# HGRN scores: levels 32 and 64 as separate products on three column groups, copied into A

## The chip, the cores and the metric

The kernel runs on one core of one Trainium2 chip. The metric is the device time of one execution in microseconds. A core has a tensor engine (PE, whose weight loads are listed apart as PEld), a vector engine (DVE), a scalar engine (ACT), GpSimd (POOL) and a sync engine (SP) that here issues the weight transfers. Each engine takes its own instructions in a fixed order, and semaphores tie the engines together.

## The reference, cut to what matters

The reference is a two-layer decoder for one sequence of 256 tokens of width 1024. Layer 0 mixes tokens with a gated linear recurrence (HGRN2), layer 1 with a three-branch sparse attention; each is followed by a SwiGLU feed-forward, and conditioning vectors made from `c` scale, shift and gate every sub-layer. The change touches the recurrence alone:

```python
def step(state, inp):
    G = jnp.cumsum(g_, axis=2)
    o_inter = einsum(q_ * exp(G), state)
    decay = where(causal, exp(G[t] - G[s]), 0)        # per key feature
    attn = einsum('bhtk,bhsk,bhtsk->bhts', q_, k_, decay)
    o_intra = einsum(attn, v_)
    new_state = exp(G_last) * state + einsum(k_ * exp(G_last - G), v_)
```

For each of 8 heads the result is one causal 256 by 256 score matrix times the values. A score of query t and key s is the sum over 128 features of q, k and the product of all decays between s and t.

## The kernel before, in words

The kernel does not run the recurrence chunk by chunk. It splits the causal triangle by levels 1, 2, 4, ..., 128. At level b the tokens are cut into blocks of 2b; queries in the second half of a block meet keys in its first half, and the decay between them is a product of one factor per key and one per query, both measured from the middle of the block. So at each level the scores are plain matrix products of a scaled key tile with a scaled query tile. `hgrn_decays` makes those tiles `X[0]` to `X[7]` (and `X[8]` for the diagonal) with exponentials on ACT (line 786, recorded under `act` at line 429) and running sums on DVE (lines 790 to 792). `hgrn_scores` (line 793) takes a group of two heads and makes the products; `hgrn_values` (line 841) multiplies by the values.

The four groups are called S0 to S3 in the written order of the stage, with D0 and D1 the decays of two groups each, `i` value products, `g` gate products, V0 and V1 the products with the values: `D0 i0 g0 S1 i1 S0 V0 D1 g1 S2 S3 i2 i3 V1`.

Inside one group there are four tiles of 128 by 128 scores on the diagonal (two heads times two halves of the tokens, index `ht`) and two tiles below it (level 128, tile `psx`, line 825). For a diagonal tile the scores inside blocks of 32 are made with 32-column products on four column groups of PE (lines 807 and 813, tile `psl`), masked and merged by DVE into `ab` (lines 827 and 834), and spread by a DVE product with a block mask into the block diagonal of `A` (line 838). Levels 64 and 32 go to a second accumulator tile, `psu`: a product of a cleared bf16 tile with itself opens the accumulation over all 128 by 128 places (line 817), then the level-64 product (line 818), two level-32 products (line 821), then a second product with the cleared tile, two columns wide, that closes the accumulation (line 824). DVE adds the whole of `psu` to `A` (line 839). ACT copies `psx` into `A[:, 4:6]` (line 840). An fp32 product shows as two weight loads and two matmuls in the trace.

Accumulators for all these (`psl`, `psu`, `psx`, `hgpv`, `hgt`, `adat`) come from one ring of four banks (`m_tile`, line 491). The order of instructions on each engine is made by a planner from the program's order, its own cost estimates and the priorities in `PRI`; the program text fixes dependencies, not the final order. Around the scores PE also runs value products (`hg_i`, lines 748 to 750), gate products (`hg_g`, lines 484 to 486) and conditioning vectors (`adapsg`, `adapsss`, line 385). Weights are streamed by SP in chunks of 1 MB, four ahead, and split into two parts by ACT (line 307, `wh`) and DVE (line 308, `wl`).

Of the kernel before, what the change touches and what calls it, by code (L numbers as in the profile page):

```python
# [21 lines left out]
S = 256  # L22
D = 1024
# [4 lines left out]
RAW = 4  # chunks loaded ahead  # L28
DEFER = 3  # chunks of a feed-forward's first product taken before rstd is there
XBUFS = 14  # L30
XMOD, XOFF = 5, 9  # every how many halves of a chunk go to the second ring, and until which chunk
PTS = 3  # pairs of heads with probabilities at a time
QACT, KACT = 0x0F, 0xF0  # chunks of the queries' and values' input made on ACT
CSTK = 7  # chunk after which the rest of the constants is loaded
# how far ahead of the program (behind it, if negative) some of the work is issued
# [7 lines left out]


# conditioning vectors (s shift and scale, g gate) on the tensor engine; the others are row sums on DVE
# [11 lines left out]
# The order of the work. hgrn: D decays, S scores, i/g products, V values. nsa: q queries, G gates, c compression,  # L57
# n norms, w values, x compressed softmax, s scores, v outputs, a conditioning chunk.
# hada, f0, f1: after how many chunks of products each conditioning chunk comes.
# [115 lines left out]
def row_constants():  # L175
    """Row 32 m + h of column block m: ones on the partitions of half h."""
    r = np.zeros((P, 4, P), np.float32)
    for m in range(4):
        for h in range(2):
            r[32 * m + h, m, 64 * h:64 * h + 64] = 1.0  # L180
    return r.reshape(P, 4 * P)


def first(name):
    """What the method issues is moved by PRI in the order of the program."""
    def wrap(f):
        def g(self, *a, **k):
            n = PRI.get(name, 0)
            if not n:
                return f(self, *a, **k)  # L190
            with self.tc.high_priority(offset=n):
                return f(self, *a, **k)
        return g
    return wrap


class K:
# [154 lines left out]
    def ada(self, kind, l, i, t):  # L352
        """Two columns of 128 conditioning values: rows of the chunk against c."""
        nc = self.nc
        m, A, bias = self.ada_tiles(l)
        c0, c1 = (i, 8 + i) if kind == "ada_ss" else (16 + 2 * i, 17 + 2 * i)
        for h, c in enumerate((c0, c1)):
            junk = self.tp.tile([P, D], F32, tag="junk", bufs=1, name="junk")
            nc.vector.tensor_tensor_reduce(out=junk, in0=t[:, h * D:(h + 1) * D], in1=self.crep, scale=1.0,  # L359
                                           scalar=0.0, op0=ALU.mult, op1=ALU.add, accum_out=m[:, c:c + 1])  # L360
        if kind == "ada_ss":
            gain = self.col(self.gain(l))
            nc.vector.scalar_tensor_tensor(A[:, i:i + 1], m[:, c1:c1 + 1], self.bias1(l)[:, c1:c1 + 1],
                                           gain[:, i:i + 1], op0=ALU.add, op1=ALU.mult)
            nc.vector.tensor_tensor(m[:, i:i + 1], m[:, i:i + 1], bias[:, i:i + 1], op=ALU.add)
            if i == 7:
                self.mods[("A", l)] = A
                self.mods[("shift", l)] = m[:, 0:8]
        else:
            nc.vector.tensor_tensor(m[:, c0:c1 + 1], m[:, c0:c1 + 1], bias[:, c0:c1 + 1], op=ALU.add)  # L370
            if i == 3:
                self.mods[("gate", l)] = m[:, 16:24]

    def ada_pe(self, kind, l, i, t):
        """c against the chunk's rows, summed over the chunks; at the last one the columns."""
# [43 lines left out]
    def act(self, out, in_, func, **kw):  # L419
        """An activation whose function lies in a table set; sets change only between phases."""  # L420
        nc = self.nc
        want = 18 if func == AF.Silu else 6
        if want != self.aset:
            load = nc.scalar.add_instruction(mybir.InstLoadActFuncSet(
                act_func_set_id=want, name=nc.get_next_instruction_name(), engine=nc.scalar.engine, ins=[], outs=[]))
            for i in self.aphase:
                self.after(load, i)
            self.aset, self.aload, self.aphase = want, load, []
        r = nc.scalar.activation(out, in_, func, **kw)  # L429
        self.after(r, self.aload)  # L430
        self.aphase.append(r)
# [6 lines left out]
    def rsqrt_cols(self, v, n, tag):  # L438
        """v ** -0.5 for a few columns, by Newton's method from the exponent."""
# [11 lines left out]
    def rsqrt(self, v, shape, tag):  # L451
        """(v + EPS) ** -0.5, one Newton step after the tables."""
# [13 lines left out]
    def sigmoid(self, out, v, shape):  # L466
        """exp(min(v, 0)) / (1 + exp(-|v|))"""
# [26 lines left out]
    def gemm(self, ps, w, hh, hl, n=256):  # L494
        """ps = sum over k of w[k] (128 x 128) against h[:, k, :n]."""
# [3 lines left out]
    def tiles(self, w):  # L499
        """The 128 x 128 tiles of half a chunk: high and low parts."""  # L500
        return [(w[0][:, e * P:(e + 1) * P], w[1][:, e * P:(e + 1) * P]) for e in range(8)]
# [6 lines left out]
    def set_shift(self, hh, hl, l):  # L508
        """Columns 256 and 257 of the moving operand: the shift vector and zeros."""
# [14 lines left out]
    def stat(self, x, m):  # L524
        """Adds the squares of chunk m to the sum over chunks."""
# [10 lines left out]
    def first_stat(self):  # L536
        """rstd of the input."""
# [25 lines left out]
    def stat_end(self, ps=None):  # L563
        """self.rstd = (mean of squares + EPS) ** -0.5 of every token, on all partitions."""
# [17 lines left out]
    def full_chunk(self, hh, hl, m, A, sh, pool):  # L582
        """Chunk m of x * rstd * A + shift, in two parts."""
# [7 lines left out]
    def full_pair(self, which, l, xr, pool, on_act):  # L591
        """The same from x * rstd."""
# [22 lines left out]
    def gemm_deferred(self, ws, h, pool, name, ub=2):  # L615
        """Products with h as it is before rstd: their values times rstd, and the shift's column."""
# [17 lines left out]
    def residual(self, ps, m, gate, nxt):  # L634
        """x_new chunk m = x + gate * y, with what the next products need of it."""
# [20 lines left out]
    def hgrn(self):  # L656
# [3 lines left out]
        with self.tc.tile_pool(name="hg", bufs=1) as gp, self.tc.tile_pool(name="hg2", bufs=2) as g2:  # L660
# [17 lines left out]
            # room of the next operands until their first parts are there  # L678
# [62 lines left out]
    def gemm_tok(self, ps, h, ws):  # L741
        """Tokens on the partitions: h (stationary) against the weights."""
# [9 lines left out]
    def hgrn_decays(self, fs, qs, g2):  # L752
        """X[l]: exp of the log decay from each block's middle; left keys, right queries. X[8]: keys."""
# [41 lines left out]
    def hgrn_scores(self, X, q, g2, i):  # L795
        nc = self.nc
        # scores inside blocks of 32, all levels side by side
# [3 lines left out]
        for h in range(2):  # L801
            for tt in range(2):
# [6 lines left out]
                for l, b in enumerate(LOW):  # L809
                    for j in range(4):  # L810
# [4 lines left out]
                                         tile_position=(0, 32 * j))  # L815
                u = psu[:, ht]
                nc.tensor.matmul(u, lhsT=self.zero, rhs=self.zero, start=True, stop=False)
                nc.tensor.matmul(u[0:64, 64:128], lhsT=X[6][:, h, base:base + 64],
                                 rhs=X[6][:, h, base + 64:base + 128], start=False, stop=False)
                for j in (0, 64):  # L820
                    nc.tensor.matmul(u[j:j + 32, j + 32:j + 64], lhsT=X[5][:, h, base + j:base + j + 32],
                                     rhs=X[5][:, h, base + j + 32:base + j + 64], start=False, stop=False,
                                     tile_position=(0, j))
                nc.tensor.matmul(u[:, 0:2], lhsT=self.zero, rhs=self.zero[:, 0:2], start=False, stop=True)
# [14 lines left out]
        nc.vector.tensor_tensor(A[:, 0:4], A[:, 0:4], psu, op=ALU.add)  # L839
# [3 lines left out]
    def hgrn_values(self, ns, As, v, g2, q):  # L843
        """Into q: rms-normalised rows of A^T v times the gain, features on the partitions."""
# [75 lines left out]
    def raw_heads(self, ps, name):  # L920
        """Products of two column tiles off the accumulator, and their squares."""
# [7 lines left out]
    def rotate(self, u, gain, swap, kr, name):  # L929
        """kr = the rotation of u times the gain: halves of a head change places."""  # L930
# [11 lines left out]
    def head_norm(self, pairs, kr, gain=None, kn=None):  # L942
        """Four column tiles: kr times the heads' rstd, kn = u times that and the gain."""
        nc = self.nc
        ps = self.m_tile([P, S], "hs")
        # rows 32 e and 32 e + 1: the two heads of column tile e
# [124 lines left out]
    def cmp_blocks(self, sw, u, kind, Dt, pool):  # L1071
        """Dt[(parity, d), i, (head, block)]: token 16 block + 2 i + parity of a head, plus its position."""
# [160 lines left out]
    def attend_values(self, j):  # L1233
# [4 lines left out]
        for half in range(2):  # L1238
            for br in range(2):
                PT[half, br] = self.pt_tile(f"PT{j}_{half}{br}")  # L1240
                pt = self.pp.tile([P, 3, P], F32, tag="acc", bufs=3, name="ptt")
                # columns: keys 0 with tokens 0, keys 0 with tokens 1, keys 1 with tokens 1
# [27 lines left out]
def _kt(w):  # L1270
    """[K, M] -> [128, K / 128, M]"""
# [3 lines left out]
def head_order():  # L1275
    """Query heads by (column tile, half): halves of a tile use key heads 2 g and 2 g + 1."""
# [107 lines left out]
```

## Time and profile before

| what | value |
|---|---|
| median of 3 runs | 765.33 us (764.39 to 766.17) |
| span of the profiled execution | 764.0 us |
| PE busy | 736.8 us, 96% of the span, 6580 products |
| DVE busy | 573.1 us, 75% |
| ACT busy | 395.2 us, 52% |
| share of the critical chain on PE | 88% |
| mean granted TensorE clock | 0.988 |

The page gives no other time for the profiled execution than its span, from the first to the last instruction. A row of the timeline gives start, duration, engine, line, operation, output and inputs, shape, count, and in brackets the idle time before it. A matmul's duration runs from its start to a modelled end, so starts that follow one another closely tell the rate, not the durations. "Issue" in the chain is time in which the engine waited for nothing that the profile shows. [...]

### The profile page before, as it was taken

What the parts mean: (1) busy time and instruction counts of PE and PEld (TensorE: products, weight loads), DVE (VectorE), ACT (ScalarE), POOL (GpSimd) and SP (SyncE); (2) the same over time, 40 slices, a digit from 0 to 9 for tenths busy, and PEclk for the clock granted to TensorE, in tenths of its full rate; (3) what the DMA queues carried; (4) which work ended last, traced back from release to release, by engine and by line L of the source; (5) the groups of instructions that cost most, each with busy time, mean ns of one, the idle gap of its engine ahead of it and who ended that gap; (6) DMA issues with size and microseconds to landing.
All of it is one profiled execution on the core that took longest, in us unless ns stands there. A gap on an engine that the chain in (4) does not pass through costs nothing.

```text
span 764.0 us, 15991 instructions
## 1 busy us (share of the span) xinstructions
PE 736.8 (96%) x6580; PEld 671.6 (88%) x6580; DVE 573.1 (75%) x1231; ACT 395.2 (52%) x746; POOL 0.6 (0%) x7
## 2 busy tenths in 40 slices
PE   3999999899999999999999899999999999999997
PEld 1999986689999999999996787555799999999997
DVE  5996988469898988987598869668489757565631
ACT  4339856357644544544474644558466444444330
POOL 0000000000000000000000000000000000000000
PEclk9999999799999999999999999999999999999999
DMA  8999745475489796887733942552755555755710
GB/s 330 335 341 355 274 133 210 139 284 203 143 320 377 275 366 266 333 333 285 274 112 97 359 134 74 173 215 109 275 204 182 208 179 206 275 203 205 266 39 21
DMA packets 26571, 174.13 MB, mean 228 GB/s; under 512 B 3201, under 2 KB 4609, under 8 KB 6018
## 3 DMA queue, kind: packets, MB, share of 16 engines
q1 hardware_dynamic: 24912, 170.80, 60.7%
q10 hardware_dynamic: 1586, 2.32, 1.1%
q8 instruction: 51, 0.84, 0.4%
q14 instruction: 22, 0.18, 0.1%
HBM read 170.48 MB, written 1.05 MB: 225 GB/s over the span
## 4 chain that ended last, share of the span: by engine, by line
PE 88%; DVE 5%; ACT 3%; DMA 2%; issue 1%; ACTq 0%; DVEq 0%
PE ff L486 11%; PE ff L485 11%; PE ff L484 11%; PE ffo L484 6%; PE ffo L485 5%; PE ffo L486 5%; PE adapsss L385 2%; PE po L1260 2%; PE ptt L1244 2%; PE s L1207 2%; DVE wl L308 1%; PE q L485 1%; PE nso L484 1%; PE hg_i L748 1%; PE hgo L484 1%; PE q L486 1%
## 5 line engine op out<-in xcount | busy, mean ns | idle before, releaser
L308 DVE TENSOR_TENSOR wl<-raw,wh 128x1024 fp32r<-128x1024 f32 x201 | 244.0, 1222 | 72.7 <-ACT wh L307 72.2
L307 ACT CAST wh<-raw 128x1024 fp32r<-128x1024 f32 x201 | 208.7, 1048 | 152.8 <-PE ff L485 53.0
L486 PE MATMUL ff<-hh,wl 128*128 128x256 f32 (+1 forms) x704 | 198.3, 282 | 0.0
L484 PE MATMUL ff<-hh,wh 128*128 128x256 f32 (+1 forms) x704 | 198.1, 282 | 0.0
L485 PE MATMUL ff<-hl,wh 128*128 128x256 f32 (+1 forms) x704 | 198.1, 282 | 0.0
L486 PEld LDWEIGHTS ff<-hh,wl 128*128 128x128 f32 x704 | 133.1, 189 | 0.0
L485 PEld LDWEIGHTS ff<-hl,wh 128*128 128x128 f32 x704 | 132.7, 189 | 0.3
L484 PEld LDWEIGHTS ff<-hh,wh 128*128 128x128 f32 x704 | 132.6, 189 | 0.1
L484 PE MATMUL ffo<-gh,wh 128*128 128x256 f32 x352 | 99.0, 282 | 0.6 <-DVE x L638 0.6
L485 PE MATMUL ffo<-gl,wh 128*128 128x256 f32 x352 | 98.6, 280 | 0.0
L486 PE MATMUL ffo<-gh,wl 128*128 128x256 f32 x352 | 98.5, 280 | 0.0
L359 DVE CUSTOM_DVE_ANT_0 junk<-raw,crep 128x1024 f32<-128x1024 f32 x64 | 78.1, 1220 | 2.8 <-DMA raw<-in_w 2.2
L484 PEld LDWEIGHTS ffo<-gh,wh 128*128 128x128 f32 x352 | 66.0, 188 | 1.3 <-DVE x L638 1.0
L486 PEld LDWEIGHTS ffo<-gh,wl 128*128 128x128 f32 x352 | 66.1, 188 | 0.0
L485 PEld LDWEIGHTS ffo<-gl,wh 128*128 128x128 f32 x352 | 66.1, 188 | 0.0
L479 ACT CAST gh<-fg 128x256 fp32r<-128x256 f32 x44 | 17.8, 405 | 42.0 <-DVE fg L894 41.4
L429 ACT ACTIVATE Pt<-Pt,nm 128x128 f32<-128x128 f32 x64 | 28.2, 442 | 9.8 <-DVE nm L1215 9.8
L480 DVE TENSOR_TENSOR gl<-fg,gh 128x256 fp32r<-128x256 f32 x44 | 18.6, 422 | 8.2 <-ACT gh L479 8.2
L587 ACT ACTIVATE hh<-t,mod 128x256 fp32r<-128x256 f32 x24 | 11.4, 505 | 24.6 <-DVE t L586 24.6
L429 ACT ACTIVATE fs<-ff 128x256 f32<-128x256 f32 x38 | 14.5, 380 | 15.3 <-PE ff L486 15.3
L638 DVE SCALAR_TENSOR_TENSOR x<-ffo,mod,x 128x256 f32<-128x256 f32 x16 | 7.7, 482 | 18.9 <-PE ffo L486 18.9
L385 PE MATMUL adapsss<-raw,c 128*32 128x512 f32 x128 | 21.1, 632 | 0.8 <-issue 0.8
(324 smaller groups left out, 1497.8 us busy)
## 6 DMA issues: line engine op xcount, KB each, us to landing
raw<-in_w SPq DMA_DIRECT2D x160, 1024.0 KB, 5.6
x<-in_x SPq DMA_DIRECT2D x2, 512.0 KB, 5.0
usq<-huq ACTq DMA_DIRECT2D x16, 64.0 KB, 2.4
out<-x SPq DMA_DIRECT2D x8, 128.0 KB, 1.9
cst<-in_cst ACTq DMA_DIRECT2D x1, 558.0 KB, 7.7
usk<-huk ACTq DMA_DIRECT2D x8, 64.0 KB, 3.9
raw<-in_w SPq DMA_DIRECT2D x1, 512.0 KB, 4.3
rselr<-in_rsel SPq DMA_DIRECT2D x1, 256.0 KB, 2.9
```

The lines of the kernel that those rows point to most:

```text
L307: nc.scalar.copy(wh, u)
L308: nc.vector.tensor_tensor(wl, u, wh.bitcast(F32), op=ALU.subtract)
L359: nc.vector.tensor_tensor_reduce(out=junk, in0=t[:, h * D:(h + 1) * D], in1=self.crep, scale=1.0, scalar=0.0, op0=ALU.mult, op1=ALU.add, a ...
L385: nc.tensor.matmul(self.aps[32 * j:32 * j + 32, :q], lhsT=self.c32[:, k], rhs=t[:, n * D + j * q:n * D + (j + 1) * q], start=k == 0, stop= ...
L429: r = nc.scalar.activation(out, in_, func, **kw)
L479: self.nc.scalar.copy(hi, v)
L480: self.nc.vector.tensor_tensor(lo, v, hi.bitcast(F32), op=ALU.subtract)
L484: mm(ps, lhsT=wh, rhs=hh, start=first, stop=False)
L485: mm(ps, lhsT=wh, rhs=hl, start=False, stop=False)
L486: mm(ps, lhsT=wl, rhs=hh, start=False, stop=last)
L1207: nc.tensor.matmul(ps, lhsT=self.QR[hs, j, tt * P:tt * P + P], rhs=self.KR[hs, g, :, 0:n], start=True, stop=True)
L1244: nc.tensor.transpose(pt[:, e], Pt[half][:, br, e * P:(e + 1) * P], self.c("ident"))
```

## The change

`hgrn_scores` no longer uses the cleared tile. Both products with it are gone. The level-64 product and the two level-32 products each start and stop an accumulation of their own, with explicit places on the column groups: level 64 on columns 0 to 63, level 32 on columns 64 to 95 and then on columns 0 to 31 (the order of the two is turned round). The parts of `psu` that no product writes are left unwritten. The DVE addition of `psu` to `A` is replaced by three ACT copies of the written blocks into `A`, over what the mask product of line 838 left there. Line numbers stay the same but for the replaced lines; comments are dropped.

```diff
@@ hgrn_scores
                 u = psu[:, ht]
-                nc.tensor.matmul(u, lhsT=self.zero, rhs=self.zero, start=True, stop=False)
                 nc.tensor.matmul(u[0:64, 64:128], lhsT=X[6][:, h, base:base + 64],
-                                 rhs=X[6][:, h, base + 64:base + 128], start=False, stop=False)
-                for j in (0, 64):
+                                 rhs=X[6][:, h, base + 64:base + 128], start=True, stop=True,
+                                 tile_position=(0, 0))
+                for j in (64, 0):
                     nc.tensor.matmul(u[j:j + 32, j + 32:j + 64], lhsT=X[5][:, h, base + j:base + j + 32],
-                                     rhs=X[5][:, h, base + j + 32:base + j + 64], start=False, stop=False,
+                                     rhs=X[5][:, h, base + j + 32:base + j + 64], start=True, stop=True,
                                      tile_position=(0, j))
-                nc.tensor.matmul(u[:, 0:2], lhsT=self.zero, rhs=self.zero[:, 0:2], start=False, stop=True)
...
         nc.vector.tensor_tensor(a4, ab[:, :, None, :].to_broadcast([P, 4, 4, 32]), bm, op=ALU.mult)
-        nc.vector.tensor_tensor(A[:, 0:4], A[:, 0:4], psu, op=ALU.add)
+
+        for p, n, t in ((0, 64, 64), (0, 32, 32), (64, 32, 96)):
+            nc.scalar.copy(A[p:p + n, 0:4, t:t + n], psu[p:p + n, :, t:t + n])
         nc.scalar.copy(A[:, 4:6], psx)
         return A
```

## Rows read from the trace of the kernel before

**Rows 1.** The page: busy time of each engine, the chain's shares, and the instruction queue of PE (packets, MB, share).

```profile
PE 736.8 (96%) x6580; PEld 671.6 (88%) x6580; DVE 573.1 (75%) x1231; ACT 395.2 (52%) x746; POOL 0.6 (0%) x7
...
q8 instruction: 51, 0.84, 0.4%
...
PE 88%; DVE 5%; ACT 3%; DMA 2%; issue 1%; ACTq 0%; DVEq 0%
```

**Rows 2.** All instructions on the tile `psu`: count, then minimum, median and maximum duration in ns, first and last start in us.

```profile
L818 PE MATMUL psu<-s x32: 222/270/369, 96.7 to 142.6; 128*64 128x64 f32 x32
L817 PE MATMUL psu<-zero x16: 216/230/288, 79.9 to 142.2; 128*128 128x128 bf16 x16
L824 PE MATMUL psu<-zero x16: 177/178/185, 97.2 to 143.1; 128*128 128x2 bf16 x16
L839 DVE TENSOR_TENSOR A<-A,psu x4: 677/680/687, 106.0 to 148.9; 128x512 f32<-128x512 f32 x4
```

**Rows 3.** PE's timeline in S1, where the four diagonal tiles' `psu` products follow one another.

```profile
97.16 0.18 PE L824 MATMUL psu<-zero 128*128 128x2 bf16 x1
97.20 0.22 PE L817 MATMUL psu<-zero 128*128 128x128 bf16 x1
97.35 0.33 PE L818 MATMUL psu<-s 128*64 128x64 f32 x2
97.61 0.26 PE L821 MATMUL psu<-X 128*32 128x32 f32 x4
97.79 0.18 PE L824 MATMUL psu<-zero 128*128 128x2 bf16 x1
```

**Rows 4.** PE's timeline in S0, where `psl` and `psu` products of a tile alternate.

```profile
101.16 0.23 PE L817 MATMUL psu<-zero 128*128 128x128 bf16 x1
101.32 0.33 PE L818 MATMUL psu<-s 128*64 128x64 f32 x2
101.57 0.26 PE L821 MATMUL psu<-X 128*32 128x32 f32 x4
101.76 0.18 PE L824 MATMUL psu<-zero 128*128 128x2 bf16 x1
101.87 0.27 PE L807 MATMUL psl<-q,X 128*32 128x32 f32 x8
```

**Rows 5.** ACT's and DVE's timelines around the assembly of A in S0 and the decays D1, and PE's first level-64 product of S2 with DVE's last step before it.

```profile
106.88 0.38 ACT L840 COPY A<-psx 128x256 f32<-128x256 f32 x1 [4.22 <-PE psx L825]
107.45 1.77 ACT L429 ACTIVATE X<-rf 128x512 f32<-128x512 f32 x3 [0.20 <-DVE rf L763]
...
109.53 0.68 DVE L838 TENSOR_TENSOR A<-ab,cst 128x512 f32<-128x512 f32 x1
...
128.05 0.42 DVE L792 TENSOR_TENSOR s<-s,q 128x256 f32<-128x256 f32 x1
...
128.61 0.30 PE L818 MATMUL psu<-s 128*64 128x64 f32 x2
```

**Rows 6.** The chain of waits in order of time: the two pieces in which PE stood idle (start, length, what).

```profile
132.09 0.84 issue
...
136.89 2.05 issue
```

**Rows 7.** Busy time by stretch (start and end, length, then busy time and count of PE, PEld, DVE, ACT, POOL, granted clock, DMA share, GB/s): first from a boundary to the end of the first idle stretch, from there to the end of the second; then two stretches that the prediction uses.

```profile
127.70:132.90 5.20, 4.26 (x148) 3.01 (x141) 4.51 (x13) 3.04 (x4) 0.00 (x0) 1.00 0.61 255
132.92:138.93 6.01, 3.97 (x128) 2.80 (x127) 2.74 (x7) 4.44 (x7) 0.00 (x0) 0.97 0.52 177
...
127.85:134.24 6.39, 5.42 (x156) 3.54 (x148) 4.86 (x14) 2.93 (x5) 0.00 (x0) 1.00 0.61 219
134.24:139.29 5.05, 3.00 (x149) 2.46 (x146) 2.26 (x5) 4.40 (x7) 0.00 (x0) 0.93 0.44 178
```

**Rows 8.** The same view of the stretches after the second idle stretch.

```profile
138.90:143.90 5.00, 4.96 (x109) 3.78 (x112) 1.09 (x3) 0.04 (x1) 0.00 (x0) 0.50 0.01 3
143.90:148.80 4.90, 4.90 (x24) 2.99 (x26) 4.73 (x9) 0.48 (x2) 0.00 (x0) 0.50 0.41 119
148.80:154.00 5.20, 5.20 (x42) 4.32 (x37) 0.74 (x2) 1.03 (x8) 0.00 (x0) 0.99 0.84 310
```

**Rows 9.** PE's timeline in S3 after the second idle stretch, and the first product with the values of S2.

```profile
139.60 0.29 PE L817 MATMUL psu<-zero 128*128 128x128 bf16 x1
...
140.48 0.18 PE L824 MATMUL psu<-zero 128*128 128x2 bf16 x1
140.60 0.33 PE L807 MATMUL psl<-q,X 128*32 128x32 f32 x8
...
145.72 0.80 PE L854 MATMUL hgpv<-v,A 128*128 128x128 f32 x2
...
154.09 0.38 PE L854 MATMUL hgpv<-v,A 128*128 128x128 f32 x2
```

**Rows 10.** ACT's and DVE's timelines where the last two groups' A are assembled, and the two ACT forms nearest to the new copies.

```profile
148.69 0.28 ACT L859 ACTIVATE osq<-hgpv 128x128 f32<-128x128 f32 x1 [4.36 <-PE hgpv L856]
...
142.57 0.68 DVE L839 TENSOR_TENSOR A<-A,psu 128x512 f32<-128x512 f32 x1
...
148.16 0.69 DVE L838 TENSOR_TENSOR A<-ab,cst 128x512 f32<-128x512 f32 x1
...
L859 ACT ACTIVATE osq<-hgpv x16: 269/278/322, 114.5 to 156.5; 128x128 f32<-128x128 f32 x16
L840 ACT COPY A<-psx x4: 372/372/375, 100.7 to 144.0; 128x256 f32<-128x256 f32 x4
```

## The prediction

> **What bounds the kernel now.** Read the page's busy shares first: PE is busy 96% of the span and carries 88% of the chain that ended last [rows 1]. So an edit is worth what it takes from PE's order of work, plus what it does to PE's waits; DVE (75%) and ACT (52%) count only where PE waits for them. Next read the instructions on `psu`: 16 pairs of products with the cleared tile, 32 records of level 64, and four DVE additions of 0.68 us [rows 2]. Their durations overlap, so the price of a product is read from starts, in the timeline of PE [rows 3, 4]. [...]
>
> **The two stops are instruction fetch.** The second stop ends at 138.93, the first at 132.92; between them PE starts 128 products and 127 weight loads [rows 7], which with one recorded semaphore wait is 256. The instruction queue of PE moves 0.84 MB in 51 packets, 16.5 KB each, and 51 packets for 2 x 6580 instructions are 258 a packet [rows 1]. So PE takes instructions in blocks of 256, and the stops stand at block ends. Counting 256 back from the first stop puts a block end at 127.70 (the first window's counts include the thirty-odd still in flight at its start). From that end to the first resumption are 5.2 us, from there to the second 6.0 us [rows 7]. I read these as the time to get the next block while weights stream. Here a block holds only 3 to 4 us of work.
>
> **Removed on PE, S1 and S0 (8 diagonal tiles).** Where tiles follow one another (S1), the starts go 97.16 (closing), 97.20 (opening), 97.35 (level 64), 97.61 (level 32), 97.79 (closing) [rows 3]: 0.63 us a tile. The slots of the two cleared products are 0.04 + 0.15 = 0.19 us; the 0.18 from level 32 to the closing product is partly the change from 32 to 128 columns, which a change from 32 to 64 may keep. So the saving is 0.19 to 0.37; I take 0.25, near the lower end, because a change of shape stays. In S0 the block from opening product to the next `psl` product is 101.16 to 101.87, 0.71 us [rows 4]; what stays is level 64 to level 32, 0.25, and at least a few hundredths for the four 32-column records. The saving is between 0.15 + 0.11 = 0.26 and 0.40; I take 0.35, since 32 columns follow 32 columns. Sum 4 x 0.25 + 4 x 0.35 = 2.4 us, ends 1.8 and 3.1. [...]
>
> **What of it arrives at S2.** PE's first level-64 product of S2 starts at 128.61, and DVE's last step on its input ran from 128.05 to 128.47 [rows 5]: PE has hardly any slack against the decays D1. D1 alternates between ACT exponentials and DVE. DVE loses two additions of 0.68 (1.36 us) before then [rows 2]. ACT gets six copies. None of their shapes is in the trace; the nearest are 0.37 us for 128x256 and 0.28 for 128x128 [rows 10], so a group's three copies cost 0.37 + 2 x 0.28 = 0.93 us, between 0.6 (their starts overlap) and 1.1 (three of the larger). ACT had 4.22 us idle before 106.88 [rows 5], which covers S1's set; S0's set stands among D1's exponentials. So the head start at S2 lies between 0.3 (DVE's 1.36 less a 1.1 us delay of ACT) and 2.4 (PE's own). I take 1.6, DVE's gain and part of waits that become shorter.
>
> **S2 and S3, as far as the fetch decides.** The stretch from one block end to the next keeps 256 instructions, but now without cleared products. Each removed product is two instructions; with 34 gone before (32 of S1 and S0, and S2's first opening pair), the first block end moves to the instruction now at 127.85, the next, 14 removals on, to 134.24, the third, 8 on, to 139.29 (the counts of those windows, 304 and 295, hold some 30 in flight at each edge) [rows 7]. Old time over the two blocks: 6.39 + 5.05 = 11.44 us. Natural work without the stops: 6.39 - 0.84 - 0.8 = 4.75 (14 removals are three and a half tiles) and 5.05 - 2.05 - 0.7 = 2.3 us (two tiles). Both are under the fetch times of 5.2 and 6.0, so the new time is 11.2 and the saving 0.24, I take 0.3. PE would stop for about 0.5 and 3.7 us instead of 0.84 and 2.05. Ends: if both fetches took 6.0, a loss of 0.6; if none held PE, a gain of 4.5.
>
> **The last two tiles of S3.** [...] One block goes from 139.60 to 140.60, 1.00 us [rows 9]; the opening product's 0.22 and the closing one's 0.12 are sure, 0.3 more depends on the shape change. I take 0.45 each, 0.9 in all (0.7 to 1.3).
>
> **A through ACT.** The new copies follow line 838 and replace line 839, 0.93 for 0.68 us plus a change of engine. For S2 the addition ends at 143.25 and the product with the values starts at 145.72; for S3 line 838 ends at 148.85, the copies by about 150, and the product starts at 154.09 [rows 9, 10]. Cover is 2.5 and 4 us, so I cost it at nothing; without cover it would be 0.3 to 0.5 us a group. Queued behind the copies on ACT are the squares of S2 (148.69), for which DVE's norm waits, and that waits for S3 anyway. The banks of `psu` come free when the copies end. No DMA is added and SP's queue passes nothing; its transfers move with the work.
>
> **Sum.** 1.6 + 0.3 + 0.9 = 2.8 us off the span of 764.0. The runs lie 0.4 to 2.2 us above that span with a median of 765.33, so I set the change against the median: 762.5 us. The low clock I leave as long as it was.
>
> **Rivals.** *B, the fetch is in time and PE keeps its clock.* After 138.94 the weight queues were idle (DMA share 0.01 [rows 8]); if the new rhythm puts the fetches into such a lull, the stops (0.84 + 2.05) go, S2 and S3 give their full 0.8 + 0.7 + 0.9, and without the stop the clock need not fall, worth half of 9.9 us, 4.95. With the 1.6 before: 11.9 us (6.9 and 4.95), 753.5; with the stops gone but the clock falling, 758.4. For it: DVE and ACT have slack in S3. Against it: weights streamed at a DMA share of 0.61 and 0.52 in both blocks [rows 7]. [...]
>
> *C, nothing arrives.* PE's head start is waited away before S2 (0.3 left), the longer second stop eats 0.3, and the last tiles give 0.7: 0.7 us, 764.6. For it: PE's 0.14 us of slack at 128.61. Against it: DVE really loses work there.
>
> *D, slower.* The copies of S0 stand on ACT directly behind the copy at 106.88, ahead of D1's three exponentials at 107.45, and wait there for DVE's line 838, which ends at 110.21 [rows 5]. ACT takes its instructions in order, so the exponentials start at 110.21 + 0.93 = 111.1 instead of 107.45, up to 3.6 us later. Less DVE's 1.36 that is 2.3 us, and PE waits at S2 instead of arriving early. [...] It decides from about 2.8 us of delay on. For it: ACT's order is planned by costs that do not know when `ab` is ready. Against it: line 840's own wait of 4.22 us did not hold up exponentials before, and a plan that puts line 838 late puts the copies late too.
>
> **How the numbers follow.** Forecast 0.50, B 0.14 (0.05 of it with the clock kept), C 0.20, D 0.16. About 0.2%, 1.5 us, is what a measurement tells from no change, so faster means under 763.8. The forecast lies under that with nine tenths of its chance, 0.45, and B adds 0.14: faster 0.59. C and the rest of the forecast: same 0.25. D: slower 0.16. The likeliest case alone runs from 760.5 (full 2.4 at S2, 1.3 at the end, 1 from the fetch) to 764.5 (0.6 arrives, the fetch costs 0.6, 0.7 at the end). The range of 8 in 10 takes in B with the fallen clock and much of D, and leaves out B with the clock kept and D's far end: 758.0 to 767.0.
>
> **What would show it.** Right: 32 products fewer on PE; starts of `psu` 0.4 us apart from tile to tile in S1; six ACT copies before 115 us without a wait of over 1 us; two stops of PE 256 instructions apart in S2 and S3, the second the longer, together about 4 us, then some 10 us at 0.50. Wrong: no stop between 125 and 140 (B); S2's first level-64 product not earlier than 128.3 (C) or later than 129 with ACT waiting for line 838 ahead of exponentials (D); a changed order of work elsewhere, outside 90 to 160 us, that moves more than a microsecond.

## The result, and the profile after

The changed kernel takes 758.7 us (756.62 to 761.92, 20 runs) beside 764.66 us (759.4 to 766.17, 20 runs) for the kernel before on the same chip: ratio 0.9927, interval 0.9915 to 0.994, by the ratio about 5.6 us less. The forecast was 762.5 with a range of 758.0 to 767.0. Direction and range held, but the gain is twice the 2.8 us of the sum. The profiled execution of the changed kernel took 761.92 us, the slowest of its 20. So differences of stages are read below from five profiles: two of the kernel before (its first one and the run "e12_before_again"), and three of the changed one (the first, "e11_changed_again", and "e3_old_places", whose order of work is the same).

The page of the changed kernel, with the lines that answer to [rows 1]:

```profile
PE 733.0 (96%) x6548; PEld 669.4 (88%) x6548; DVE 570.3 (75%) x1227; ACT 398.7 (52%) x758; POOL 0.6 (0%) x7
...
q8 instruction: 51, 0.84, 0.4%
...
PE 85%; DVE 8%; ACT 3%; DMA 2%; issue 1%; ACTq 0%; DVEq 0%
```

PE has 32 products fewer, DVE four operations fewer and ACT twelve more, as written. The instructions on `psu` (columns as in [rows 2]; lines behind 839 have moved by two):

```profile
L822 PE MATMUL psu<-X x64: 189/217/263, 96.6 to 137.7; 128*32 128x32 f32 x64
L818 PE MATMUL psu<-s x32: 222/270/369, 96.3 to 137.4; 128*64 128x64 f32 x32
L841 ACT COPY A<-psu x12: 249/256/365, 104.7 to 144.2; 32x128 f32<-32x128 f32 x8, 64x256 f32<-64x256 f32 x4
```

PE's timeline in S1, which answers to [rows 3]:

```profile
96.33 0.33 PE L818 MATMUL psu<-s 128*64 128x64 f32 x2
96.59 0.26 PE L822 MATMUL psu<-X 128*32 128x32 f32 x4
96.78 0.33 PE L818 MATMUL psu<-s 128*64 128x64 f32 x2
97.04 0.26 PE L822 MATMUL psu<-X 128*32 128x32 f32 x4
97.22 0.33 PE L818 MATMUL psu<-s 128*64 128x64 f32 x2
```

Level 64 starts every 0.45 us (96.33, 96.78, 97.22) where a tile took 0.63: 0.18 a tile.

The level-64 products of S0's last two tiles, which answer to [rows 4], and the first one of S2, which answers to the last of [rows 5]:

```profile
102.29 0.33 PE L818 MATMUL psu<-s 128*64 128x64 f32 x2
...
103.16 0.33 PE L818 MATMUL psu<-s 128*64 128x64 f32 x2
...
126.19 0.33 PE L818 MATMUL psu<-s 128*64 128x64 f32 x2
```

In the kernel before, the level-64 product behind that of [rows 4] in S0 is this one:

```profile
102.58 0.33 PE L818 MATMUL psu<-s 128*64 128x64 f32 x2
```

So a tile of S0 takes 0.87 us from one level-64 product to the next (102.29, 103.16), where it took 1.26 (101.32 [rows 4], 102.58). The planner's order differs a little too: in S0 and S2 the `psl` products of two tiles now stand ahead of the first level-64 product, where it was one tile in S0 and all four in S2.

ACT's timeline where A is assembled, for S1, S0, S2 and S3 in turn:

```profile
104.74 0.78 ACT L841 COPY A<-psu 64x256 f32<-64x256 f32 x3
...
109.49 0.79 ACT L841 COPY A<-psu 64x256 f32<-64x256 f32 x3
110.30 0.69 ACT L429 ACTIVATE X<-rf 128x512 f32<-128x512 f32 x1
...
138.32 0.79 ACT L841 COPY A<-psu 64x256 f32<-64x256 f32 x3 [4.44 <-DVE A L838]
...
143.66 0.77 ACT L841 COPY A<-psu 64x256 f32<-64x256 f32 x3
```

A group's three copies take 0.77 to 0.79 us (forecast 0.93, bounds 0.6 to 1.1). S0's set stands among the exponentials (line 429) and has no idle time before it; only S2's set waits, 4.44 us for DVE's line 838, and what stands behind it on ACT is the copy of `psx` into the same A.

The chain of waits, the pieces in which PE stood idle (they answer to [rows 6]):

```profile
130.18 1.19 issue
...
134.03 1.61 issue
```

Busy time by stretch (columns as in [rows 7]): the two blocks, each from its end on PE to the resumption after it, then the second idle stretch and what follows it, which answers to [rows 8]:

```profile
126.98:131.37 4.39, 3.20 (x136) 2.60 (x136) 3.72 (x10) 3.33 (x5) 0.00 (x0) 1.00 0.65 226
131.37:135.64 4.27, 2.66 (x128) 2.30 (x129) 1.28 (x5) 2.19 (x3) 0.00 (x0) 0.60 0.47 196
...
134.00:135.60 1.60, 0.03 (x2) 0.00 (x0) 0.00 (x0) 0.00 (x0) 0.00 (x0) 0.50 0.00 0
135.60:139.00 3.40, 3.36 (x72) 1.99 (x72) 1.57 (x5) 0.67 (x3) 0.00 (x0) 0.50 0.02 5
139.00:144.00 5.00, 5.00 (x35) 2.71 (x35) 4.31 (x8) 2.77 (x13) 0.00 (x0) 0.99 0.38 103
```

Again 256 instructions lie between the stops, and again PE's granted clock falls there, to a mean of 0.60 over the second block and 0.50 behind it. But the two blocks now take 4.39 and 4.27 us, 8.7 together, where they took 5.2 and 6.0 [rows 7]. PE's products fill 3.20 and 2.66 us of them.

A table of five profiles, each time counted from the first level-64 product of S1, in us (from the starts in the trace; the last line adds up the pieces before the first `rb` in which the granted clock was 0.50, called half clock):

| to | before | before again | changed | changed again | old places |
|---|---|---|---|---|---|
| last `psx` of S0 | 9.85 | 10.03 | 7.82 | 7.60 | 7.91 |
| first `psl` of S2 | 29.86 | 30.05 | 28.95 | 29.17 | 29.04 |
| first level 64 of S2 | 31.89 | 32.09 | 29.86 | 30.07 | 29.94 |
| last level 64 of S3 | 45.89 | 44.79 | 41.07 | 41.35 | 41.45 |
| first `rb` of the feed-forward | 101.65 | 99.13 | 96.01 | 97.44 | 97.34 |
| of this at half clock | 10.24 | 3.41 | 6.83 | 10.24 | 6.83 |

By the means of the columns, S1 and S0 give 2.2 us, of which 0.9 is left at S2's first `psl`; by the end of S3 the lead is 4.1. (S2's first level 64 is 2.0 earlier, but with fewer `psl` products ahead of it.) At the first `rb`, with half of the half-clock time taken off each figure (an estimate, from the granted 0.50), the lead is some 4.0 (97.0 less 92.9). From there on the order of work is the same in both kernels.

### The profile page after: what moved, and what is told of

The parts are those of the page before. It is cut to its first block, busy times and chain, and to the rows that moved or that the text cites. A ratio compares the mean times of both kernels' runs of the same rounds, so it can differ in the third digit from the quotient of the medians.

```text
span 760.1 us, 15934 instructions
## 1 busy us (share of the span) xinstructions
PE 733.0 (96%) x6548; PEld 669.4 (88%) x6548; DVE 570.3 (75%) x1227; ACT 398.7 (52%) x758; POOL 0.6 (0%) x7
## 3 DMA queue, kind: packets, MB, share of 16 engines
HBM read 170.48 MB, written 1.05 MB: 226 GB/s over the span
## 4 chain that ended last, share of the span: by engine, by line
PE 85%; DVE 8%; ACT 3%; DMA 2%; issue 1%; ACTq 0%; DVEq 0%
PE ff L486 11%; PE ff L485 11%; PE ff L484 11%; PE ffo L484 5%; PE ffo L485 5%; PE ffo L486 5%; DVE wl L308 3%; PE po L1262 2%; PE adapsss L385 2%; PE ptt L1246 2%; PE s L1209 2%; PE q L485 1%; PE q L486 1%; PE nso L484 1%; PE hgo L484 1%
## 5 line engine op out<-in xcount | busy, mean ns | idle before, releaser
L1213 DVE CUSTOM_DVE_ANT_0 Pt<-s,cst 128x128 f32<-128x128 f32 (+1 forms) x64 | 19.0, 351 | 3.3 <-PE s L1209 3.3
```

Of the source, the lines that this page charges most:

```text
L1213: nc.vector.tensor_tensor_reduce(out=Pt[half][:, br, o:o + n], in0=ps[:, br], in1=cs[:, S - n:], scale=1.0, scalar=-3e38, op0=ALU.add, op1 ...
```

## The experiments

Each was timed beside the kernel before. One of them is the kernel before against itself: its interval reaches to 1.0029, so a difference of 0.3% is the least that is told apart here, and more where an interval is wider.

**Parts of the change.** The cleared products stay, and only DVE's addition is replaced:

```diff
-        nc.vector.tensor_tensor(A[:, 0:4], A[:, 0:4], psu, op=ALU.add)
+        for p, n, t in ((0, 64, 64), (0, 32, 32), (64, 32, 96)):
+            nc.scalar.copy(A[p:p + n, 0:4, t:t + n], psu[p:p + n, :, t:t + n])
```

> Both products with the cleared tile stay and only DVE's addition is replaced by the three ACT copies. If the gain comes from PE's products (theory A), the ratio is 0.998 to 1.003 and S2's first level-64 product comes no more than 1 us earlier than before. If it comes from DVE's lost additions and the new order (theory B), the ratio is 0.993 to 0.996.

Measured: 763.01 us beside 764.46, ratio 0.9983 (0.9963 to 1.0004). Taking 2.7 us off DVE is worth 1.3 us by the ratio while PE's work stays, and the interval takes in both nothing and 2.8. S2's first `psl` product starts 30.22 us after the first level 64 of S1, no earlier than in the kernel before (29.86 and 30.05 in the table).

Next the changed kernel with its copies on DVE:

```diff
-            nc.scalar.copy(A[p:p + n, 0:4, t:t + n], psu[p:p + n, :, t:t + n])
+            nc.vector.tensor_copy(A[p:p + n, 0:4, t:t + n], psu[p:p + n, :, t:t + n])
```

> The products as changed, but the three copies of psu into A are made by DVE. Theory A: the ratio to the kernel before is 0.992 to 0.996, as for the changed kernel. Theory B (what counts is that DVE is relieved): 0.996 to 1.000, since DVE now has about 0.2 us more to do a group than with the addition.

Measured: 765.94 beside 764.46, ratio 1.0026 (1.0003 to 1.005). With 32 products fewer this kernel is no faster than before, some 7 us behind the same change with copies on ACT, and outside what either theory had (0.992 to 1.000). A line of DVE's timeline shows what a group's copies cost there, against 0.68 us for the addition [rows 2], and one of the chain a wait that the changed kernel does not have:

```profile
103.32 0.91 DVE L841 COPY A<-psu 64x256 f32<-64x256 f32 x3
...
116.82 5.03 DMA raw<-in_w
```

In this profile PE waits 2.3 us at `adapsss` (line 385) for a chunk of weights that came late. The planner's order differs as well: the last value products (`hg_i`) stand behind S3, where the changed kernel has them ahead of S2. So the run compares more than the engine of the copies. The one trace is of the fastest of its 12 executions (762.85 us, where the slowest took 771.22), and what makes the loss in the others was not shown.

Then the old places and order of the three products, the rest as changed:

```diff
-                                 rhs=X[6][:, h, base + 64:base + 128], start=True, stop=True,
-                                 tile_position=(0, 0))
-                for j in (64, 0):
+                                 rhs=X[6][:, h, base + 64:base + 128], start=True, stop=True)
+                for j in (0, 64):
```

> As changed, but level 64 without an explicit place and level 32 in the old order, columns 0 to 31 first. If the column groups running side by side give part of the gain, S1's step from tile to tile is 0.05 to 0.1 us longer than in the changed kernel and the ratio about 0.001 higher. If only the lost products count, the step and the ratio are those of the changed kernel.

Measured: 759.04, ratio 0.9927 (0.9909 to 0.9945). S1's level-64 products start at 96.21, 96.65 and 97.09, no further apart than in the changed kernel. The explicit places and the order are worth nothing that could be told apart.

**Does the place of the block ends decide?** Products with the cleared tile, two columns wide, are put at the very start, their result unused. PE runs 64 of them between 1.2 and 2.9 us, when it would wait for weights. Nothing else of PE's order changes; only the block ends move, by 128 instructions.

```diff
+        pad = self.m_tile([P, P], "pad")
+        for _ in range(64):
+            nc.tensor.matmul(pad[:, 0:2], lhsT=self.zero, rhs=self.zero[:, 0:2], start=True, stop=True)
         self.issue(RAW)
```

> The changed kernel with 64 two-column products of the cleared tile (128 PE instructions) put at the very start, where PE waits for the input anyway. If the two stops of PE in S2 and S3 are ends of blocks of 256 instructions, both move 128 instructions up in the program, so that the first falls about where 2881 and 3137 instructions of the changed kernel have run (near 129 and 133.5 us), or one goes away; the ratio to the kernel before stays within 0.990 to 0.998. If they are something of the products themselves, they stay at the same products.

Measured: 770.48, ratio 1.0083 (1.006 to 1.0105), nearly 12 us more than the changed kernel. Its chain of waits, PE's idle pieces:

```profile
91.74 3.99 issue
...
107.15 3.67 issue
...
138.18 3.01 issue
...
148.32 0.70 issue
```

The stops stand after 1729, 2241, 3009 and 3521 instructions of PE, at steps that are multiples of 256, and are now 11.4 us together. The expected 0.990 to 0.998 was missed by far: the stop at 3009 is where it was expected (2881 instructions of the changed kernel), the next one is gone, but two new ones stand ahead, and one behind, in places where the changed kernel did not stop. The same pad in the kernel before:

> The kernel before with the same 128 PE instructions ahead as in e4. Theory F says that before loses as well when its block ends fall at a bad place: ratio 1.006 to 1.014, stops at counts 1729, 2241 and 3009, and the change is then worth 0 to 4 us against e4's 770.5. If the place of the block ends is of no account to the kernel before, the ratio is 0.998 to 1.002.

Measured: 779.11, ratio 1.022 (1.018 to 1.026). Stops of 3.72, 2.66 and 4.05 us stand after 1729, 2241 and 3009 instructions, and behind the last PE is at half clock for 20.5 us, as its busy time by stretch shows (columns as in [rows 7]):

```profile
141.00:146.00 5.00, 4.73 (x63) 3.35 (x63) 1.27 (x2) 0.00 (x0) 0.00 (x0) 0.50 0.01 3
146.00:151.00 5.00, 5.00 (x103) 2.96 (x105) 2.56 (x8) 1.98 (x5) 0.00 (x0) 0.50 0.59 213
...
156.00:161.00 5.00, 5.00 (x25) 2.93 (x26) 4.42 (x10) 0.37 (x1) 0.00 (x0) 0.50 0.15 25
```

With this pad the change is worth 779.11 less 770.48, 8.6 us (by the two ratios some 10), more than the 0 to 4 that were expected, and the ratio is above the expected 1.006 to 1.014. The stops of the two padded kernels are about as long together (10.4 us here, 11.4 in the changed one), but the time at half clock in the recurrence is 30.7 us here and 17.1 in the changed one. Half the pad in the changed kernel (`range(32)`):

> The changed kernel with 32 further two-column products of the cleared tile with itself at the start, 64 PE instructions, half as many as in the run that took 770.5 us; nothing else of PE's order moves. The result of the pad is used by nothing. Theory one, the place of the block ends decides: stops at counts 1729, 2241, 3009 and 3265, estimated by a model that gives every fetch 4.4 to 5.2 us, of 2.0, 2.3, 1.6 and 1.0 us, 7 us in all against 2.8 in the changed kernel, a mean clock of 0.986 to 0.990 and a time of 762 to 766 us, ratio 0.998 to 1.003. Theory two, the pad of 64 products cost its time by itself, by being there at the start: half the pad gives half its cost, 764.6 us, but with stops of half the size of those at the same counts and no new clock loss. Theory three, anything under a block is free: 758 to 760 us.

Measured: 766.59 beside 764.26, ratio 1.0036 (1.0018 to 1.0055). The idle pieces in its chain, after 1729, 2241 and 3009 instructions:

```profile
94.41 2.79 issue
...
107.14 2.91 issue
...
137.20 2.37 issue
```

They are 8.1 us together where 7 were estimated, and the fourth is missing. Each is over half of its like under the full pad (3.99, 3.67, 3.01), so theory two's halving fails. The time is 0.6 us above theory one's range and 2.0 above theory two's figure: three of the four stops stand where theory one put them, its model is too mild. Theory three, that less than a block is free, is out.

**The change where nothing stops.** In both kernels the levels 2 to 16 are left out of the products and of the merging on DVE (the same edit in both loops), so that a block of 256 instructions holds more time:

```diff
-                for l, b in enumerate(LOW):
+                for l, b in enumerate(LOW[:1]):
```

> The kernel before without the products and merges of levels 2, 4, 8 and 16 (left out of the computation), so that the score groups hold a quarter of their PE instructions and no block of 256 runs out early. Together with e6 it measures what the change is worth without stops at block ends. Alone: no stop of PE longer than 0.3 us at a block end between 90 and 140 us, ratio 0.975 to 0.99.

> The changed kernel thinned in the same way. If the change's gain is the PE time of the removed products (theory A), e6 is 2.5 to 6 us under e5. If most of the gain comes from where the block ends fall (theory F), e6 is 0 to 2.5 us under e5.

Measured: 751.28 (ratio 0.9848) and 747.13 (0.9806). No stop is left in either chain, and the mean clock is 0.998 and 0.996. The change is worth 4.15 us here by the medians of five runs each, and 3.2 by the ratios, whose intervals overlap (0.9811 to 0.9886, 0.9769 to 0.9842). So its own work, without the stops, is some 3 to 4 us; the runs do not give it more closely.

**Long products among the short ones.** The third group of gate products is put ahead of S3 in the changed kernel (the lines that carry out `h2` are left out here):

```diff
-        "D0 i0 g0 S1 i1 S0 V0 D1 g1 S2 S3 i2 i3 V1"
+        "D0 i0 g0 S1 i1 S0 V0 D1 g1 S2 i2 i3 h2 S3 V1"
```

> The changed kernel with the third gate product put ahead of S3 in the program, so that 48 long products stand between the dense blocks of S2 and S3. If stops at block ends and the clock's fall after them are what is left there, the second stop shrinks below 0.8 us or goes and the ratio to the kernel before falls to 0.986 to 0.991. If the planner's other order costs as much elsewhere, 0.991 to 0.996.

Measured: 757.39 (753.59 to 759.62), ratio 0.9918 (0.9886 to 0.9951). In S2 and S3 the stops of 1.19 and 1.61 shrink to one of 0.85, the mean clock is 0.9965, and part of it is paid back where the values wait for A, as the chain shows:

```profile
137.57 0.85 issue
...
141.90 0.69 DVE hl L480
...
142.81 0.29 issue
143.09 0.46 PE hgpv L858 x2
```

The 0.29 us of issue behind that wait stand after 3522 instructions, within one of the next block end, so a fetch may have a share in that wait. The stop of 0.85 is a little above the 0.8 that were expected. It is the best median of the kernels that compute everything, but its interval covers the changed kernel's ratio. With the fourth group of gate products moved as well, to directly behind S3 (`S3 h3 V1`):

> The changed kernel with the third and the fourth group of gate products both moved, one ahead of S3 and one behind it, where nothing but value products stood. Theory one, the recurrence loses time where a block of 256 short products lasts less than its fetch: long gate products among the short ones make the blocks of S3 last longer than a fetch, so no stop of over 0.5 us in S3, a mean clock of 0.997 or more, and a time of 756 to 758 us, ratio to the kernel before 0.989 to 0.993. Theory two, only the number of instructions ahead counts and not what the block holds: stops at counts of 3009 and 3265 PE instructions as in the changed kernel, 1.2 and 1.6 us, a time of 758 to 760 us. If the gate products are missed later (they wait for weights that are not yet there, or the values wait for A), PE waits 1 to 2 us behind S3 and the time is 759 to 761 us.

Measured: 760.74, ratio 0.9956 (0.9942 to 0.9971). PE's waits between 85 and 200 us (what waits, for what, us in total, times, longest):

```profile
PE hgt L871 <- DVE o L868: 2.8, 3, 1.7
PE adapsss L385 <- issue: 2.5, 1, 2.5
PE hgo L484 <- ACT hh L479: 1.3, 1, 1.3
```

The stops at 3009 and 3265 are gone, as theory one had it, but the next block end, 3521, now falls behind short products and stops PE for 2.5 us, and the moved products are missed as cover for the norm. The third case, 759 to 761, is the one that came.

**Both kernels once more**, for a second profile of the clock.

> The changed kernel once more, beside the two others on the same chip: 758 to 760 us, ratio 0.991 to 0.994, stops at counts 3009 and 3265. If its time at half clock is what differs from run to run, its runs spread over 756 to 762 us along with their mean clock.

> The kernel before once more, for a second look at where its time at half clock lies. Theory one, the half clock in the recurrence belongs to the kernel and that behind 390 us falls by chance in each execution: 10.2 us at half clock behind the second stop again, stops again at counts of 3009 and 3265 PE instructions (0.8 and 2.1 us), but another number of 3.4 us stretches between 390 and 455 us, where the first profile had two. Theory two, the later stretches belong to the kernel too: two of them again, at the same places within a microsecond or two. Either way the time is 763 to 766 us, ratio 0.998 to 1.002.

Measured: 758.54 beside 764.26 (0.9934, 0.9909 to 0.9958), and 765.16 beside 764.11 (1.0015, 1.0000 to 1.0029). The stops are after 3009 and 3265 instructions in each, 1.25 and 1.13 us in the changed kernel (which also stops for 0.70 us after 2241), 1.23 and 1.50 in the one before. Busy time by stretch (columns as in [rows 7]) in the first profile of the kernel before:

```profile
137.00:147.00 10.00, 8.05 (x119) 5.22 (x120) 4.48 (x11) 2.31 (x4) 0.00 (x0) 0.58 0.09 13
...
419.00:429.00 10.00, 7.56 (x61) 5.39 (x58) 7.21 (x14) 7.30 (x16) 0.00 (x0) 1.00 0.83 318
```

The same stretches in its second profile:

```profile
137.00:147.00 10.00, 9.45 (x141) 5.95 (x142) 6.51 (x13) 2.62 (x11) 0.00 (x0) 0.83 0.28 92
...
419.00:429.00 10.00, 7.77 (x50) 7.11 (x47) 7.99 (x10) 7.43 (x12) 0.00 (x0) 0.83 1.01 424
```

The granted clock behind the stops is 0.58 in one execution and 0.83 in the other, 10.2 and 3.4 us at half clock, with the same program. So theory one was wrong in its first half: not even the half clock in the recurrence belongs to the kernel as a fixed length. The later 3.4 us stretches number two in both profiles, where theory one wanted another number. One begins at 408 us in the first and at 403 in the second, in which everything is 3.9 us earlier by then, the other at 449 and at 423; so theory two holds for one of them and fails for the other; the three profiles of the changed order have three, none and one.

## Why the prediction was right, and where it was too small

The direction, the stops and the products that the gain comes from were right; the gain forecast was half of the one measured. The 758.7 us lie below the 760.5 to 764.5 of the likeliest case alone. The range reached down to 758.0 because of rival B with the fallen clock (758.4), in which both stops go, and they stayed. So it is in part luck that the range held.

*What bounds the kernel, and the stops as fetch:* right, as far as the traces show it. Block ends 256 instructions apart kept their places in five profiles, and a pad that runs while PE would wait for weights moved the stops and cost 8 to 15 us. In the changed kernel's profile 48 of 50 block ends pass without a stop of over 0.3 us, and the two in S2 and S3 stop PE for 1.19 and 1.61; with the pads such a stop took up to 4.05 us.

*S1 and S0:* 2.4 forecast, 2.2 measured: 0.18 a tile in S1, just below the lower end of 0.19, and so some 0.36 a tile in S0 (2.2 less 0.7, over four), where the step between the last two tiles fell by 0.39. The step from level 32 to the next product in S1 is 0.18 us before (97.61 to 97.79 [rows 3]) and 0.18 to 0.19 after; that a change of shape is a part of it was my estimate, and no run separates it.

*What arrives at S2:* 1.6 forecast, 0.9 measured at the first `psl`, inside its ends. The reason given, DVE's lost additions, is not borne out: in e1, where they alone go, S2's first `psl` starts no earlier than in the kernel before. As far as that one trace tells, the 0.9 came from PE's own products.

*S2 and S3 as far as the fetch decides, and the last two tiles:* this is the step that failed. I gave the two blocks 11.2 us, since their fetches had taken 5.2 and 6.0, and so a saving of 0.3, with 0.9 for the tiles behind them: 1.2. From S2's start to the last level 64 of S3 the table shows 4.1 less 0.9, 3.2 us. (The end of 4.5 for a saving without stops should read 4.4: 11.44 less 4.75 and 2.3.) The error is that I took the length of a fetch from one execution as a constant. From block end to resumption the two blocks take 5.2 and 6.0, then 5.6 and 5.5 in the kernel before; they take 4.4 and 4.3, 4.4 and 4.3, and 5.2 and 3.7 in the changed order. In all ten PE resumes 2.2 to 2.5 us after the instruction queue begins to move the packet; what varies is the time until it begins, 1.3 to 3.6 us after the block end.

In these profiles that time follows the weight stream. Busy time by stretch (columns as in [rows 7], the DMA share is the last but one) in the kernel before, from a block end to the packet's start, from there to the resumption, then the same for the second block, and last from the second resumption to the packet after it:

```profile
127.70:130.60 2.90, 2.77 (x137) 2.22 (x130) 2.51 (x8) 1.86 (x4) 0.00 (x0) 1.00 1.02 429
130.60:132.93 2.33, 1.49 (x36) 0.79 (x23) 2.02 (x5) 1.17 (x1) 0.00 (x0) 1.00 0.10 35
132.93:136.49 3.56, 3.56 (x117) 2.51 (x116) 1.83 (x6) 2.00 (x5) 0.00 (x0) 1.00 0.85 290
136.49:138.94 2.45, 0.40 (x16) 0.29 (x12) 0.90 (x3) 2.45 (x4) 0.00 (x0) 0.93 0.04 13
138.94:140.06 1.12, 1.11 (x40) 0.96 (x40) 0.00 (x0) 0.00 (x0) 0.00 (x0) 0.50 0.00 0
```

The changed kernel's two waits for the packet and the resumption after the second, and the second block of e1:

```profile
126.98:129.01 2.03, 2.03 (x110) 1.76 (x110) 2.03 (x6) 1.45 (x2) 0.00 (x0) 1.00 0.86 363
131.37:133.40 2.03, 2.03 (x100) 1.78 (x104) 1.28 (x5) 1.71 (x3) 0.00 (x0) 0.72 0.95 404
133.40:135.64 2.24, 0.63 (x42) 0.52 (x37) 0.00 (x0) 0.48 (x1) 0.00 (x0) 0.50 0.03 7
...
133.47:134.52 1.05, 1.05 (x53) 0.89 (x57) 0.08 (x1) 0.32 (x2) 0.00 (x0) 1.00 0.14 39
```

In all ten cases the packet starts as the transfer of weights in flight runs out, within 0.8 us of it. (In the other runs some packets start earlier than that, a few in the middle of a running stream.) Where hardly any weights move, it starts 1.1 us after the block end: behind the second stop in all five profiles, and in e1, whose PE work in S2 and S3 is that of the kernel before and whose second stop is gone. So in the ten cases a fetch took the time until the weights in flight were through and 2.2 to 2.5 us more. In the changed order that time was 1.3 to 2.9 us, in the kernel before 2.9 to 3.6. No run moved the weights alone, so it is read from traces and not tested that the packet waits behind them, and why the chunks lay better for the changed kernel stays open.

PE's own work in the two blocks was smaller as well, 3.20 and 2.66 us where I had 4.75 and 2.3: two long `adapsss` products that I had counted in now stand elsewhere. So the stops stayed at 2.4 to 3.7 us together (2.7 and 2.9 in the kernel before) instead of growing to 0.5 and 3.7, and the removed products gave their own time.

*The low clock, left as it was:* right for the recurrence, as far as five profiles tell (10.2 and 3.4 against 6.8, 10.2 and 6.8 us), but over many runs not quite. The 77 runs of the kernel before whose clock is on record (the 20 beside the first result have none) have a mean of 764.0 us at a mean clock of 0.990; 32 of the changed order have 758.9 at 0.9925. At one and the same mean clock, 0.993, ten runs of before average 762.7 and 13 of the changed order 758.5: 4.1 us less. So of 5.1 us some 4 are work, and about 1 is less time at half clock. Charging each run half of its half-clock time instead gives 3.2 and 1.9. The 4 agree with the table, and the 3 to 4 with the thin pair. Where the last microsecond of the clock is saved is open.

*A through ACT at nothing:* right for the copies themselves, but the reason was too narrow. The reason was PE's cover; with the copies on DVE all the gain was lost, so the engine matters too. That ACT's idle time is what made the change pay is argued, not shown, since that run's order of work differs as well.

*The rivals.* B, fetch in time and clock kept, did not come in this kernel, as both stops stayed; the thin pair and the moved third group of gate products show what it supposes, a mean clock of 0.996 or more where the stops go or shrink to one of 0.85, and e1 shows a fetch in a lull of the weights that costs PE nothing (DMA share 0.14, PE busy for all of the 1.05 us). C fell with the lead of some 4 us at the first `rb`. D fell on ACT's timeline: S0's copies do not stand right behind the copy of `psx`, but at 109.49, between exponentials, and wait for nothing. D's far end counts in a fall of the clock at S2, and no run shows what that would cost: up to the end of the first stop the granted clock was 1.00 in both kernels (127.70 to 132.90 [rows 7], 126.98 to 131.37).

## What to carry to other kernels

Where one engine runs many short instructions, count them: here PE's stops that no wait explains (1.19 and 1.61 us in the changed kernel) stood 256 instructions apart and were read as fetches. The length of one, 3.7 to 6.0 us here from block end to resumption, is to be read from more than one execution, and beside the DMA share, before it is put into a sum. An edit that removes instructions there shifts every later block end, so a part of its result can be luck of place (the pad of 64 products cost the changed kernel nearly 12 us); time it with a pad of idle instructions at the start before trusting or rejecting it. Ask too which engine takes what replaces removed work, and whether it has room at that moment: here the copies paid on ACT (758.7 us) and not on DVE (765.94 us, in another order of work).

## What the runs showed of the hardware that was not expected

32 or 64 tiny products at the start, over in 0.9 and 1.8 us while PE had nothing else to do, made the changed kernel 8 and 12 us slower, and 64 of them the kernel before 15. In the two blocks of five profiles the packet with PE's next 256 instructions started within 0.8 us of the end of the weight transfer in flight, 1.3 to 3.6 us after a block end, and 1.1 us after it where hardly any weights moved. And the time at half clock behind the same stop was 3.4 us in one execution and 10.2 in another of one program; run times of one kernel follow their mean clock, from some 757 us at 1.000 to some 766 at 0.984 for the kernel before.
